# Latent attention's feature tiles inside the loop over the tables, and the low-rank products one direction ahead

## The chip, the core and the metric

The kernel runs on one core of a Trainium2 chip. The metric is device time in microseconds (us) of one execution, the median of several runs. The engines are named as in the profile: PE (TensorE, matmuls; PEld is its weight load), DVE (VectorE), ACT (ScalarE), POOL (GpSimd) and SP (SyncE, which here issues loads). PSUM is where PE's products land.

## The reference

Two blocks run one after the other. The change lies in the projection of the first block's two layers: `h @ w_in` gives latent attention's columns (query latent of 256, key-value latent of 128, rotary key of 64) and 15 tiles of 128 columns for the recurrent branch. Those are shifted over the tokens and feed, per direction, a decay, a rate and the recurrence's tables.

```python
proj = h @ w_in[li]
c_q, c_kv, k_pe, rw = _split(proj, [Q_LORA, KV_LORA, QK_ROPE, RWKV_COLS])
y_att = _mla(c_q, c_kv, k_pe, cos, sin, ...)   # RMS norms of c_q and c_kv, rotary of k_pe
u = _centred_shift(rw, mu_prev, mu_next)       # p + mu_prev*(prev-p) + mu_next*(next-p)
r, k, v, wd_f, wd_b, ad_f, ad_b, gd = _split(u, ...)
g = sigmoid(gd) @ g2
kk = heads(k * k_k); kk = kk * rsqrt(sum(kk*kk, -1) + 1e-12)
def direction(d, wd, ad, reverse):
    decay = exp(-exp(-softplus(-(w0[d] + tanh(wd) @ w2[d])) - 0.5))
    a = sigmoid(a0[d] + ad @ a2[d])
    kd = heads(k * (1.0 + (a - 1.0) * k_a))
    y = _wkv_scan(r, decay, kd, v, kk, a, reverse)
    bonus = sum(r * kd * r_k, -1) * v
```

## The kernel before

There are T = 1040 tokens (16 of them meta tokens), padded to TP = 1044. Everything here has features on the partitions and tokens along the free axis. `proj` (line 346) is called once for each layer. A **feature tile** is 128 columns of `w_in`: `load` brings the weights through SP, `parts` splits them into a high part (ACT, `pw_hi`) and a rest (DVE, `pw_lo`), and `ftile` (372) runs 3 x 8 x 3 = 72 matmuls of 348 columns into a PSUM tile `pp_ps`. That tile takes three banks and has the tag `mm`, of which there are two buffers; everything of that size shares them (`low_ps`, `kk_ps` and so on). The two remaining banks are two buffers of the tag `tp`.

`shifted` (385) evicts such a tile through ACT into `pt`, and DVE makes the shifted tile of it with three operations: L391 (times c0), L392 and L393. `plain` (441) only evicts it.

The order of the work in a layer is this. Tiles 12 and 13 (inputs of decay and rate), and then `dirs` (520): four key tiles, each with `kk` and its square on ACT; `unit_keys` (620) with the norms of the keys (`norms`) and the scaling of all four `kk` (`scaled`, 12 `kkb` products), both inside the first r tile; then the **loop over the tables**, four features f times two directions d. In it come the r tile, and per direction the low-rank products (`low`, 560: six matmuls into `low_ps`, and a tanh on ACT) for the decay `lg` and the rate `ta`, one buffer each; POOL scales `lg` (570); a scan on DVE makes `cum` (573); ACT takes two exponentials; then POOL and DVE make the tables `AR` and `BK`, which ACT's queue writes to memory (610). `BK` has one buffer, `AR` one for each direction. The bonus (612 to 618) ends a feature. After the loop come the four value tiles, `values` (643), which writes their transposes in both orders (18 row blocks, `v_sb`, two buffers), and `latent` (437) with five feature tiles: rotary key, gate (tile 14), key-value latent and two of the query latent, with norms and the gate's nine products (`g_ps`, `g_sb`) put between them by `mid`. The recurrence (`recur`, 695) begins with loads of the tables on SP and the product `aa` on PE.

Within `proj` the build orders the instructions of each engine itself, as far as dependences allow; each engine then runs its own in that order. In the recurrence the order of PE, ACT, DVE and SP is written out by hand.

Of the kernel before, what the change touches and what calls it, by code (L numbers as in the profile page):

```python
# [172 lines left out]
class K:  # L173
# [172 lines left out]
    def proj(self, li, hi, lo, p, S, psp, feed):  # L346
# [3 lines left out]
        with self.tpool(name="p_w", bufs=2) as wp, self.tpool(name="p_u", bufs=2) as up, \  # L350
# [34 lines left out]
            def shifted(j, u, mid={}):  # L385
# [5 lines left out]
                nc.vector.tensor_scalar(u, pt[:, 1:T + 1], p["c0"][:, j:j + 1], None, ALU.mult)  # L391
# [29 lines left out]
            for t in (wd, ad):  # L421
                nc.vector.memset(t[:, T:], 0.0)
            u = shifted(12, up.tile([128, T], F32, name="u"))
            nc.scalar.activation(wd[:, :T], u, AF.Tanh)
            shifted(13, ad[:, :T])
# [4 lines left out]
            with self.tpool(name="p_k", bufs=1) as kp:  # L430
                self.dirs(li, p, S, psp, up, kp, shifted, wd, ad, lw)
            with self.tpool(name="p_v", bufs=1) as vp:
                vt = [shifted(8 + f, vp.tile([128, T], F32, name=f"vt{f}", tag=f"val{f}")) for f in range(4)]
# [3 lines left out]
    def latent(self, li, p, S, psp, up, vp, shifted, ftile):  # L437

        nc = self.nc

        def plain(cols, mid=None):
            ps = ftile(cols, mid={2: mid} if mid else {})
            pt = up.tile([128, TP + 1], F32, name="pt")
            nc.scalar.activation(pt[:, :TP].rearrange("p (q n) -> p q n", q=3), ps, AF.Copy)
            return pt[:, :T]
# [20 lines left out]
        u = shifted(14, up.tile([128, T], F32, name="u"))  # L466
        gd = vp.tile([128, T], F32, name="gd")
        nc.scalar.activation(gd, u, AF.Tanh, scale=0.5)
        nc.vector.tensor_scalar(gd, gd, 0.5, 0.5, ALU.mult, ALU.add)

        def keys_end():
            ps = psp.tile([128, 3, 512], F32, name="kp_ps", tag="mm")
            c3(lambda q, c, n: nc.tensor.matmul(ps[:, q, :n], dup, kr[:, c:c + n], start=True, stop=True))
            b = vp.tile([128, T], F32, name="kp", tag="val3")
            c3(lambda q, c, n: nc.scalar.activation(b[:, c:c + n], ps[:, q, :n], AF.Copy))
            nc.scalar.dma_start(S["ckv"][1], b)


        ck = plain([(256, 128, 0)], keys_end)
# [3 lines left out]
        def gate_end():  # L483
            for c, n in TT:
                gp = psp.tile([128, 512], F32, name="g_ps", tag="tp")
                nc.tensor.matmul(gp[:n], gd[:, c:c + n], g2, start=True, stop=True)
                gs = vp.tile([128, RW], F32, name="g_sb", bufs=2)
                nc.scalar.activation(gs[:n], gp[:n], AF.Copy)
                nc.scalar.dma_start(S["g"][c:c + n, :], gs[:n])

        def ckv_end():
# [6 lines left out]


        sq = []  # L500
        for f, mid in enumerate((gate_end, ckv_end)):
            a = plain([(128 * f, 128, 0)], mid)
            x = vp.tile([128, T], F32, name=f"cq_sq{f}", tag=f"val{f}")
            nc.scalar.activation(x, a, AF.Square)
            sq.append(x)
            nc.vector.tensor_scalar(a, a, p["qn"][:, f:f + 1], None, ALU.mult)
            nc.scalar.dma_start(S["cq"][f], a)
        rq, nrq = S["rq"], S["nrq"]
        nc.vector.memset(rq, 1.0)
        sqs = psp.tile([128, 9, 2], F32, name="sqs", tag="tp")  # L510
        for i, (c, n) in enumerate(TT):
            for f in range(2):
                nc.tensor.matmul(sqs[:n, i], sq[f][:, c:c + n], ones[:, 0:2], start=f == 0, stop=f == 1)
        nc.scalar.activation(rq[:NM, 0:1], sqs[:NM, 0, 0:1], AF.Sqrt, scale=1.0 / 256, bias=self.eps["rms"][:NM])
        nc.scalar.activation(rq[:, 1:9], sqs[:, 1:9, 0], AF.Sqrt, scale=1.0 / 256, bias=self.eps["rms"])
# [4 lines left out]
    def dirs(self, li, p, S, psp, up, kp, shifted, wd, ad, lw):  # L520
# [9 lines left out]
        kt, kkt = [], []  # L530
        for f in range(4):
            k = shifted(4 + f, kp.tile([128, T], F32, name=f"k{f}"))
            kk = kp.tile([128, T], F32, name=f"kk{f}")
            nc.scalar.activation(kk, k, AF.Copy, scale=p["kk"][:, f:f + 1])
            sq = kp.tile([128, T], F32, name=f"kk_sq{f}", tag=("lg", "cum", "kd", "P")[f])
            nc.scalar.activation(sq, kk, AF.Square)
            kt.append(k), kkt.append((kk, sq))
        norms, scaled = self.unit_keys(kkt, psp, kp)
        AR = [kp.tile([128, 17, 2, 64], F32, name=f"AR{d}") for d in range(2)]
        for d in range(2):  # L540
            nc.gpsimd.memset(AR[d][:, 16 * d], 0.0)
        for f in range(4):
            r = shifted(f, up.tile([128, T], F32, name="u"), {} if f else {0: norms, 2: scaled})
            k, kk = kt[f], kkt[f][0]
            kds = []
            for d in range(2):
# [3 lines left out]
                def rv(x):  # L550
                    return x[:, ::-1] if d else x
# [1971 lines left out]
```

## Time and profile before

| | us |
|---|---|
| time, median of 3 runs (lowest, highest) | 4390.14 (4386.08, 4394.14) |
| profiled execution, its own time | 4402.54 |
| its span, first to last instruction | 4400.7 |
| PE busy / DVE / ACT / POOL in the span | 3830.7 / 2767.7 / 1869.7 / 988.2 |
| PE's mean granted clock (share of 2.4 GHz) | 0.903 |

Times of a row count from the start of the span. Busy time counts instructions that run; those that wait, branch or issue a DMA are not counted. A row of the form "A <- B" says that A's engine stood idle until B released it. The granted clock is a share of 2.4 GHz, and it has two levels: 0.50 is 1.2 GHz, 1.00 is 2.4 GHz; a value between is a stretch with both. Matmuls are pipelined, so the busy time of one is more than the distance to the next.

### The profile page before, as it was taken

Reading aid. Unit: us, or ns where it says so; the run is one execution under the profiler, and the core shown is the slowest. Engines: PE = TensorE matmul, PEld = TensorE weight load, DVE = VectorE, ACT = ScalarE, POOL = GpSimd, SP = SyncE. Lnnn points to the kernel's source line nnn. Section 1 sums busy time; section 2 is a strip of 40 time slices with the busy share of each in tenths; the row PEclk is TensorE's granted clock in tenths of the full one; section 3 lists DMA queues with packets and bytes.
Section 4 is the critical chain, followed back from the end, with each engine's and each line's share of the span. In section 5 each row is a group of like instructions: output and inputs, shape, how many; then the busy total and the mean of one; then the engine's idle time right before and its main releaser. Section 6 shows DMA issues by size and latency. Waiting matters only on the chain. (4 is left out here: it accounts for less than half of the span.)

```text
span 4400.7 us, 68329 instructions
## 1 busy us (share of the span) xinstructions
PE 3830.7 (87%) x27155; PEld 3157.1 (72%) x27155; DVE 2767.7 (63%) x4684; ACT 1869.7 (42%) x3033; POOL 988.2 (22%) x719
## 2 busy tenths in 40 slices
PE   7888897899699688897887896997898889999998
PEld 7677676786576476776776775765786677888786
DVE  7763777757698757627668577997644753333354
ACT  4323445542387543233555532876424522111232
POOL 2331124201242243311233012331422410000000
PEclk9788798999799887886988997999998899999999
DMA  4446663113499833447641043998521121111232
GB/s 154 101 129 183 160 161 108 37 54 128 160 345 346 300 102 101 115 143 172 165 125 58 1 172 131 340 335 309 181 73 29 53 97 58 48 48 43 90 126 81
DMA packets 384153, 611.94 MB, mean 139 GB/s; under 512 B 50467, under 2 KB 217602, under 8 KB 381762
## 3 DMA queue, kind: packets, MB, share of 16 engines
q1 hardware_dynamic: 278402, 485.38, 35.3%
q10 hardware_dynamic: 85200, 70.97, 5.4%
q0 software_dynamic: 20224, 51.15, 3.7%
q8 instruction: 216, 3.54, 0.3%
q14 instruction: 111, 0.91, 0.1%
HBM read 491.65 MB, written 123.45 MB: 140 GB/s over the span
## 5 line engine op out<-in xcount | busy, mean ns | idle before, releaser
L252 DVE TENSOR_TENSOR w13l<-xw,w13h 128x1024 fp32r<-128x1024 f32 x248 | 296.4, 1220 | 57.5 <-ACT w13h L251 53.9
L251 ACT ACTIVATE w13h<-xw 128x1024 fp32r<-128x1024 f32 x256 | 267.4, 1058 | 130.3 <-PE x_hp L258 76.6
L256 PE MATMUL pp_ps<-T_hi,pw_hi 128*128 128x348 f32 x912 | 309.7, 340 | 8.7 <-ACT T_hi L1752 2.9
L257 PE MATMUL pp_ps<-T_lo,pw_hi 128*128 128x348 f32 x912 | 305.4, 335 | 1.4 <-DVE T_lo L1757 1.3
L258 PE MATMUL pp_ps<-T_hi,pw_lo 128*128 128x348 f32 x912 | 304.3, 334 | 0.0
L2414 PE MATMUL f_mm<-F_hi,f_wh 128*128 128x512 f32 x704 | 222.8, 398 | 1.7 <-ACT F_hi L251 1.7
L2414 PE MATMUL f_mm<-F_lo,f_wh 128*128 128x512 f32 x704 | 222.6, 397 | 0.0
L2414 PE MATMUL f_mm<-F_hi,f_wl 128*128 128x512 f32 x704 | 222.3, 397 | 0.0
L256 PE MATMUL x_hp<-w13h,x_h 128*96 128x512 f32 x512 | 208.5, 407 | 0.1
L257 PE MATMUL x_hp<-w13l,x_h 128*96 128x512 f32 x512 | 204.7, 400 | 0.0
L258 PE MATMUL x_hp<-w13h,x_l 128*96 128x512 f32 x512 | 204.0, 398 | 0.0
L256 PEld LDWEIGHTS pp_ps<-T_hi,pw_hi 128*128 128x128 f32 x912 | 179.8, 197 | 21.8 <-issue 7.8
L257 PEld LDWEIGHTS pp_ps<-T_lo,pw_hi 128*128 128x128 f32 x912 | 179.8, 197 | 5.1 <-DVE T_lo L1757 2.6
L287 POOL TENSOR_TENSOR g_x<-g_x,g2g 128x1024 f32<-128x1024 f32 x6 | 14.3, 2385 | 750.4 <-ACT g_x L284 750.4
L258 PEld LDWEIGHTS pp_ps<-T_hi,pw_lo 128*128 128x128 f32 x912 | 179.5, 197 | 3.0 <-issue 3.0
L252 DVE TENSOR_TENSOR f_wl<-F_raw,f_wh 128x1024 fp32r<-128x1024 f32 x44 | 53.7, 1221 | 203.2 <-ACT f_wh L251 203.2
L251 ACT ACTIVATE f_wh<-F_raw 128x1024 fp32r<-128x1024 f32 x44 | 46.4, 1060 | 307.0 <-PE f_mm L2414 301.4
L1616 POOL DMA_INDIRECT d_y<-x_o,r_idx x64 | 102.8, 1606 | 312.1 <-DVE x_al L252 288.8
L825 PE MATMUL aa<-ar_p,bk_p 64*128 64x128 f32 x1088 | 134.0, 376 | 40.2 <-DVE A L827 33.6
L2414 PEld LDWEIGHTS f_mm<-F_hi,f_wh 128*128 128x128 f32 x704 | 133.1, 189 | 34.4 <-ACT F_hi L251 2.0
L2414 PEld LDWEIGHTS f_mm<-F_lo,f_wh 128*128 128x128 f32 x704 | 132.7, 189 | 32.8 <-DVE F_lo L252 0.6
L2414 PEld LDWEIGHTS f_mm<-F_hi,f_wl 128*128 128x128 f32 x704 | 132.9, 189 | 32.4
(630 smaller groups left out, 11221.3 us busy)
## 6 DMA issues: line engine op xcount, KB each, us to landing
xw<-in_moe_w SPq DMA_DIRECT2D x256, 512.0 KB
xw<-in_moe_w SPq DMA_DIRECT2D x64, 1024.0 KB
wd_raw<-in_w_down SPq DMA_DIRECT2D x44, 512.0 KB
pw_raw<-in_w_in SPq DMA_DIRECT2D x36, 512.0 KB
d_AR<-AR ACTq DMA_DIRECT2D x32, 544.0 KB
d_BK<-BK ACTq DMA_DIRECT2D x32, 544.0 KB
ar_p<-d_AR SPq DMA_DIRECT2D x68, 256.0 KB
bk_p<-d_BK SPq DMA_DIRECT2D x68, 256.0 KB
```

Source lines behind the costliest of these rows:

```text
L251: nc.scalar.activation(hi, src, AF.Copy)
L252: (lo_eng or nc.vector).tensor_tensor(lo, src, hi.bitcast(F32), ALU.subtract)
L256: mm(out, wh, xh, start=first, stop=False)
L257: mm(out, wh, xl, start=False, stop=False)
L258: mm(out, wl, xh, start=False, stop=last)
L287: e1.tensor_tensor(out[:n], out[:n], gb[:n], ALU.mult)
L825: nc.tensor.matmul(aa[d][:, h - z], bk[q, h], ar[q, h], start=True, stop=True)
L1616: nc.gpsimd.indirect_dma_start(out=y2[:, :], out_offset=bass.IndirectOffsetOnAxis(ap=si, axis=0), in_=y, in_offset=None, bounds_check=2 * ...
L2414: nc.tensor.matmul(p[:, j], a[:, k], b[:, k, 512 * j:512 * j + 512], start=st, stop=sp)
```

## The change

Five things change.

- `shifted` makes its first product (times c0) on ACT, as a second reading of the PSUM tile, and no longer on DVE.
- The key tiles take the square with the scale inside; `kk` itself is made for each feature in the loop (`scaled(f)`, one DVE operation for scaling and norm), in two buffers. `norms` comes ahead of the first r tile.
- Decay and rate are made one direction ahead of their use: `lg` gets two buffers, the next `decay` is issued as a direction begins, and the next `rate` once `ta` has been used.
- A generator `compressed` makes the four latent tiles (two of the query, the key-value latent, the rotary key); the loop takes one step of it between the two directions of each feature. The unnormed key-value latent and rotary key go to a DRAM buffer `raw`, and `latent` reads them back. The query's sums of squares are taken for each tile.
- `latent` keeps one feature tile, the gate's (14); the key-value norm and the rotated key stand between its thirds.

```diff
@@ shifted
-                nc.vector.tensor_scalar(u, pt[:, 1:T + 1], p["c0"][:, j:j + 1], None, ALU.mult)
+                nc.scalar.activation(u.rearrange("p (q n) -> p q n", q=3), ps, AF.Copy, scale=p["c0"][:, j:j + 1])
+                u = u[:, :T]
@@ proj
-                self.dirs(li, p, S, psp, up, kp, shifted, wd, ad, lw)
+                self.dirs(li, p, S, psp, up, kp, shifted, wd, ad, lw, self.compressed(p, S, psp, up, cp, ftile))
@@ compressed (new; plain is ftile, eviction to pt)
+        for f in range(2):
+            a = plain([(128 * f, 128, 0)])
+            x = up.tile([128, TP], F32, name="u")[:, :T]
+            nc.scalar.activation(x, a, AF.Square)
+            sqs = psp.tile([128, 9, 2], F32, name="sqs", tag="tp")
+            for i, (c, n) in enumerate(TT):
+                nc.tensor.matmul(sqs[:n, i], x[:, c:c + n], self.ones32[:, 0:2], start=True, stop=True)
+            nc.scalar.activation(cqs[:NM, f, 0:1], sqs[:NM, 0, 0:1], AF.Copy)
+            nc.scalar.activation(cqs[:, f, 1:9], sqs[:, 1:9, 0], AF.Copy)
+            nc.vector.tensor_scalar(a, a, p["qn"][:, f:f + 1], None, ALU.mult)
+            nc.scalar.dma_start(S["cq"][f], a)
+            yield
+        for i, cols in enumerate(([(256, 128, 0)], [(384, 64, 0), (416, 32, 64), (384, 32, 96)])):
+            nc.scalar.dma_start(S["raw"][i], plain(cols))
+            yield
@@ latent
-        kr = plain([(384, 64, 0), (416, 32, 64), (384, 32, 96)])
+        ck, kr = (vp.tile([128, T], F32, name=nm) for nm in ("ck", "kr"))
+        nc.sync.dma_start(ck, S["raw"][0])
+        nc.sync.dma_start(kr, S["raw"][1])
...
-        ck = plain([(256, 128, 0)], keys_end)
...
-        for f, mid in enumerate((gate_end, ckv_end)):
-            a = plain([(128 * f, 128, 0)], mid)
...
+        u = shifted(14, up.tile([128, TP], F32, name="u"), {0: norm, 1: rotated})
...
+        for c, n in TT:
+            gp = psp.tile([128, 512], F32, name="g_ps", tag="tp")
+            nc.tensor.matmul(gp[:n], gd[:, c:c + n], g2, start=True, stop=True)
...
@@ dirs
-            kk = kp.tile([128, T], F32, name=f"kk{f}")
-            nc.scalar.activation(kk, k, AF.Copy, scale=p["kk"][:, f:f + 1])
-            nc.scalar.activation(sq, kk, AF.Square)
+            nc.scalar.activation(sq, k, AF.Square, scale=p["kk"][:, f:f + 1])
...
+            out = kp.tile([128, TP], F32, name=nm, bufs=bufs)
...
+        def decay(f, d):
+            lg = low(wd, lw["w2"], f, d, "lg", p[f"w0{d}h"], 2)
+            nc.gpsimd.tensor_scalar(lg, lg, -0.5 * CDEC, -0.5 * CDEC, ALU.mult, ALU.add)
+            return lg
+        def rate(f, d):
+            return low(ad, lw["a2"], f, d, "ta", p[f"a0{d}h"], 1)
...
+        ahead, ta1 = decay(0, 0), rate(0, 0)
+        norms()
         for f in range(4):
-            r = shifted(f, up.tile([128, T], F32, name="u"), {} if f else {0: norms, 2: scaled})
+            k, kk = kt[f], scaled(f)
+            r = shifted(f, up.tile([128, TP], F32, name="u"))
             for d in range(2):
+                lg, ta = ahead, ta1
+                if f + d < 4:
+                    ahead = decay(f + d, 1 - d)
...
                 both(lambda o, s: nc.vector.scalar_tensor_tensor(o, s[0], 0.5, s[1], ALU.mult, ALU.mult), bk, d, (rv(ta[:, :T]), cum))
+                if f + d < 4:
+                    ta1 = rate(f + d, 1 - d)
...
+                if d == 0:
+                    next(between)
@@ unit_keys
+        def scaled(f):
+            kk = kp.tile([128, T], F32, name="kk", bufs=2)
+            for c, n in NC3:
+                rb = psp.tile([128, 512], F32, name="kkb_ps", tag="tp")
+                nc.tensor.matmul(rb[:, :n], self.pairpick[:, 128 * f:128 * f + 128], rn[:, c:c + n], start=True, stop=True)
+                nc.vector.scalar_tensor_tensor(kk[:, c:c + n], kt[f][:, c:c + n], p["kk"][:, f:f + 1], rb[:, :n], ALU.mult, ALU.mult)
+            return kk
```

## Rows read from the trace of the kernel before

**Rows 1.** Windows: us; busy PE, PEld, DVE, ACT, POOL; PEclk; DMA; GB/s.
```profile
109.00:174.00 65.00, 55.52 (x231) 37.89 (x230) 47.07 (x45) 24.42 (x27) 19.35 (x12) 0.86 0.27 65
...
174.00:281.00 107.00, 83.56 (x347) 68.54 (x346) 88.79 (x80) 36.31 (x42) 59.19 (x36) 0.71 0.56 140
...
319.00:402.00 83.00, 81.66 (x499) 74.76 (x497) 18.36 (x15) 32.74 (x50) 10.11 (x8) 0.98 0.41 142
...
1649.00:1712.00 63.00, 54.81 (x227) 37.06 (x226) 45.47 (x44) 23.95 (x27) 18.93 (x11) 0.87 0.22 56
...
1712.00:1819.00 107.00, 85.59 (x350) 69.41 (x350) 86.31 (x81) 36.19 (x43) 58.13 (x36) 0.71 0.57 142
...
1901.00:1969.00 68.00, 66.99 (x403) 60.19 (x401) 11.52 (x9) 28.91 (x46) 7.86 (x7) 0.97 0.47 157
```
**Rows 2.** Windows of tile pp_ps alone: us; busy PE, PEld, ACT; PEclk.
```profile
293.00:317.00 24.00, 24.00 (x152) 24.00 (x151) 2.05 (x2) 1.00 0.29 92
...
174.00:281.00 107.00, 43.50 (x230) 42.65 (x230) 2.06 (x2) 0.71 0.56 140
```
**Rows 3.** Line L613: duration ns min/median/max, first and last start us.
```profile
L613 DVE TENSOR_TENSOR kd<-kd,u x4: 1227/1228/1229, 173.4 to 279.6; 128x1040 f32<-128x1040 f32 x4
```
**Rows 4.** Waits, 174 to 281: us in total, times, longest.
```profile
PE bo L616 <- DVE kd L613: 14.5, 2, 7.6
...
DVE cum L573 <- POOL lg L570: 7.0, 3, 3.5
...
DVE AR L595 <- ACT P L576: 6.5, 3, 3.0
...
PE low_ps L563 <- ACT pt L390: 6.2, 1, 6.2
```
**Rows 5.** PE in time: start us, us, line, tiles, count, idle before.
```profile
125.99 2.02 PE L563 MATMUL low_ps<-s_wd,r_w 64*128 64x348 f32 x6
...
132.37 1.43 PE L638 MATMUL kkb_ps<-kk_rn,pairpick 128*128 128x348 f32 x4
...
173.52 3.84 PE L563 MATMUL low_ps<-s_wd,r_w 64*128 64x348 f32 x6 [3.90 <-ACT lg L565]
...
243.54 3.72 PE L616 MATMUL bo<-rkp,kd 128*16 128x2 f32 x18 [6.82 <-DVE kd L613]
```
**Rows 6.** DVE in time at the loop's start, same columns.
```profile
125.46 6.65 DVE L632 RECIPROCAL kk_rn<-kk_rn 128x1040 f32<-128x1040 f32 x1 [1.30 <-ACT kk_rn L631]
...
132.03 1.16 DVE L252 TENSOR_TENSOR pw_lo<-pw_raw,pw_hi 128x1024 fp32r<-128x1024 f32 x1
...
133.11 0.75 DVE L391 TENSOR_SCALAR u<-pt,pc 128x1040 f32<-128x1040 f32 x1
...
149.40 1.14 DVE L639 TENSOR_TENSOR kk<-kk,kkb_ps 128x346 f32<-128x346 f32 x2 [0.32 <-PE kkb_ps L638]
...
154.91 3.42 DVE L593 SCALAR_TENSOR_TENSOR BK<-ta,cum 128x1024 f32<-128x1024 f32 x2
```
**Rows 7.** Groups by line: busy us, mean ns, idle; L610 as rows 3.
```profile
L391 DVE TENSOR_SCALAR u<-pt,pc 128x1040 f32<-128x1040 f32 x3 | 3.1, 1018 | 0.0
...
L390 ACT ACTIVATE pt<-pp_ps 128x1044 f32<-128x1044 f32 x15 | 15.4, 1026 | 7.2 <-POOL BK L590 7.2
...
L610 ACTq EVENT_SEMAPHORE  x12: 17/3132/8101, 181.2 to 276.5; - x12
```
**Rows 8.** Tail: v_sb, g_sb as rows 3; SP, PE in time.
```profile
L686 ACT ACTIVATE v_sb<-v_ps x18: 570/597/620, 328.5 to 368.2; 128x512 f32<-128x512 f32 x16, 16x512 f32<-16x512 f32 x2
...
L686 ACT ACTIVATE v_sb<-v_ps x18: 569/594/600, 1901.1 to 1936.5; 128x512 f32<-128x512 f32 x16, 16x512 f32<-16x512 f32 x2
...
L488 ACT ACTIVATE g_sb<-g_ps x9: 571/598/604, 375.7 to 398.2; 128x512 f32<-128x512 f32 x8, 16x512 f32<-16x512 f32 x1
...
393.15 0.33 SPq L305 DMA_DIRECT2D gn_g<-in_rwkv_gn_g  x1
...
402.25 0.76 PE L825 MATMUL aa<-ar_p,bk_p 64*128 64x128 f32 x2 [1.60 <-DMA bk_p<-d_BK]
```

More of the change, by code (lines that the diff above doesn't have):

```diff
@@ L460, in latent, with norm @@
         nc.sync.dma_start(g2, self.I["rwkv_g2"][li])
-        kr = plain([(384, 64, 0), (416, 32, 64), (384, 32, 96)])
+        ck, kr = (vp.tile([128, T], F32, name=nm) for nm in ("ck", "kr"))
+        nc.sync.dma_start(ck, S["raw"][0])
+        nc.sync.dma_start(kr, S["raw"][1])
         nc.gpsimd.tensor_tensor(kr[:64], kr[:64], cos[:64], ALU.mult)
         nc.gpsimd.tensor_tensor(kr[64:], kr[64:], sin[64:], ALU.mult)
[L466 to L476, printed above, removed]
-        ck = plain([(256, 128, 0)], keys_end)
         b = vp.tile([128, T], F32, name="ck_sq", tag="val2")
         nc.scalar.activation(b, ck, AF.Square)
[L483 to L491, printed above, removed]
+        def norm():
             ps = psp.tile([128, 3, 512], F32, name="ck_ps", tag="mm")
@@ L510, in latent, with rotated @@
[L510 to L515, printed above, removed]
+        def rotated():
+            ps = psp.tile([128, 3, 512], F32, name="kp_ps", tag="mm")
+            c3(lambda q, c, n: nc.tensor.matmul(ps[:, q, :n], dup, kr[:, c:c + n], start=True, stop=True))
+            k2 = vp.tile([128, T], F32, name="kp", tag="val3")
+            c3(lambda q, c, n: nc.scalar.activation(k2[:, c:c + n], ps[:, q, :n], AF.Copy))
+            nc.scalar.dma_start(S["ckv"][1], k2)
@@ new lines, in latent @@
+        u = shifted(14, up.tile([128, TP], F32, name="u"), {0: norm, 1: rotated})
+        gd = vp.tile([128, T], F32, name="gd")
+        nc.scalar.activation(gd, u, AF.Tanh, scale=0.5)
+        nc.vector.tensor_scalar(gd, gd, 0.5, 0.5, ALU.mult, ALU.add)
+        for c, n in TT:
+            gp = psp.tile([128, 512], F32, name="g_ps", tag="tp")
+            nc.tensor.matmul(gp[:n], gd[:, c:c + n], g2, start=True, stop=True)
+            gs = vp.tile([128, RW], F32, name="g_sb", bufs=2)
+            nc.scalar.activation(gs[:n], gp[:n], AF.Copy)
+            nc.scalar.dma_start(S["g"][c:c + n, :], gs[:n])
@@ L558, in both @@
                     fn(dst[:, 16 * d, slot, 0:NM], [x[:, o:o + NM] for x in srcs])
-                def low(x, wt, out, bias):
-                    ps = psp.tile([128, 3, 512], F32, name="low_ps", tag="mm")
-                    for q in range(3):
-                        nc.tensor.matmul(ps[:, q, :348], wt[64 * d:64 * d + 64, 128 * f:128 * f + 128],
-                                         x[64 * d:64 * d + 64, 348 * q:348 * q + 348], start=True, stop=True)
-                    nc.scalar.activation(out.rearrange("p (q n) -> p q n", q=3), ps[:, :, :348], AF.Tanh, scale=0.5, bias=bias)
-                lg = kp.tile([128, TP], F32, name="lg")
-                low(wd, lw["w2"], lg, p[f"w0{d}h"][:, f:f + 1])
-                nc.gpsimd.tensor_scalar(lg, lg, -0.5 * CDEC, -0.5 * CDEC, ALU.mult, ALU.add)
                 cum = kp.tile([128, T], F32, name="cum")
@@ L628, in norms @@
                 for q, (c, n) in enumerate(NC3):
-                    nc.tensor.matmul(ss[32 * f:32 * f + 32, q, :n], self.pair32, kt[f][1][:, c:c + n], start=True, stop=True)
+                    nc.tensor.matmul(ss[32 * f:32 * f + 32, q, :n], self.pair32, sqs[f][:, c:c + n], start=True, stop=True)
             for q, (c, n) in enumerate(NC3):
@@ L632, in norms @@
             nc.vector.reciprocal(rn, rn)
-        def scaled():
-            for f in range(4):
-                for c, n in NC3:
-                    rb = psp.tile([128, 512], F32, name="kkb_ps", tag="tp")
-                    nc.tensor.matmul(rb[:, :n], self.pairpick[:, 128 * f:128 * f + 128], rn[:, c:c + n], start=True, stop=True)
-                    nc.vector.tensor_tensor(kt[f][0][:, c:c + n], kt[f][0][:, c:c + n], rb[:, :n], ALU.mult)
+        def scaled(f):
[5 more added lines that the diff above has]
+            return kk
         return norms, scaled
```

59 lines of the change are left out of this document (32 added, 27 removed).

## The prediction

> **What bounds the kernel now.** The page's chain of waits does not reach back into the two projections, so I read them by stages. First the busy time by windows [rows 1]: layer 0's projection from its last key tile to the recurrence, cut where the work changes, and the same of layer 1. The reader is to see three regimes. Ahead of the recurrence (319 to 402, 1901 to 1969) PE is busy 81.7 of 83 and 67.0 of 68 us at a granted clock of 0.97 to 0.98: PE paces this stage. In the tables' loop (174 to 281, 1712 to 1819) nothing is full: DVE 88.8 of 107, PE 83.6, POOL 59.2, ACT 36.3, and PE's clock is 0.71. Between k and loop (109 to 174) PE and DVE are busy 55.5 and 47.1 of 65.
>
> Then the price of a tile where PE paces [rows 2]: 152 matmuls in 24.00 us, 0.158 us each, so 72 are 11.4 us. Then the loop's period: the last DVE step of a feature (L613) runs four times from 173.4 to 279.6 [rows 3], so 106.2 / 3 = 35.4 us per feature. What the loop waits for stands in the list of waits [rows 4]: DVE's scan for POOL's decay (7.0 us, 3 times), DVE's table product for ACT's exponential (6.5, 3 times), PE's bonus matmuls for DVE (14.5, 2 times), PE's low-rank product for ACT's eviction of a feature tile (6.2, once). It is a chain of hand-overs with no engine full, which leaves PE room but not much.
>
> **Part 1, the tail.** Four of five feature tiles leave: 4 x 11.4 = 45.5 us of PE per layer (two sums of squares go with them, not counted). That isn't the gain, for something else is late next: the value rows. v_sb is written 18 times, from 328.5 to 368.2 in layer 0 (39.7 / 17 = 2.3 us each) and from 1901.1 to 1936.5 in layer 1 (2.1 us each); g_sb's nine follow from 375.7 to 398.2 [rows 8]. Each v_sb is evicted by ACT and written out from two buffers, and ACT waits there for the write to land, so I keep this pace. Last value matmul at E = 319 (where the windows are cut): v_sb starts at E + 9.4, its 17 steps end at E + 49, the gate's nine products fit between them (now that tile 14 comes right behind the values), the recurrence's first matmul comes at about E + 50. Today it comes at 402.25 [rows 8], E + 83. **Gain 33 us.** Also gn_g's load, which stands in front of the recurrence's loads on SP, waits for the last feature matmul (393.15 [rows 8]) and moves ahead with it. In layer 1 the value chain starts at 1901.1 as today, since tile 14 takes over as filler there; it ends at 1937, plus 3 for the last gate rows: 1940 for 1969. **Gain 29 us.** Bounds: 45 if the row writes get quicker with fewer loads beside them; 22 and 18 if the gate's products queue behind all value rows (9 x 1.2 more).
>
> **Part 2, the loop.** PE gets, per feature, one more tile and six kkb matmuls (they leave the first feature). At full clock: two tiles 22.8, 24 low-rank matmuls 4 x 2.02 = 8.1, bonus 1.9 (3.72 at half clock), kkb 1.43 x 6/4 = 2.1 [rows 5]: 34.9 us. At half clock it is near double: six low-rank matmuls took 3.84. In today's loop a tile costs between: 43.5 us of PE for 230 feature matmuls [rows 2], 13.6 us a tile. With the pauses partly filled I take 12.4 a tile, 10.5 for the low-rank products (8.1 to 15.4), 2.8 for the bonus, 2.7 for kkb: 40.8. DVE per feature: 88.8 / 3 = 29.6 busy, plus pw_lo 1.2 and three kkb products 1.6 [rows 6], plus the query scale about 0.4 (L391's operation, 0.75 off the loop [rows 6], in two of four features), minus L391's 1.0 [rows 7]: 31.8. The decay's wait (2.3 per feature) goes, because lg has two buffers and is a direction ahead; the wait for the exponential (2.2) stays, for nothing is changed in front of it: 34. So PE takes over from the hand-overs as the bound of the loop, at 40.8, and I take **41 us** for the sum, with 36 (DVE paces, PE at full clock) and 53 (see below) as ends. Three features: 3 x 5.6 = +17 us.
>
> **Part 3, the loop's start.** Today the twelve kkb products of all four features run in the first direction, the last two on DVE until 150.5, and the first BK comes at 154.9, 22.8 us after the reciprocal's end (125.46 + 6.65) [rows 6]. After the change the reciprocal is the same 6.65 us, the first scan does not wait for it, and only three kk products stand behind it. PE from the last key tile (109.1): low-rank products of the first direction 4, key norms 5 (24 short matmuls; by kkb's row 8.6 at most), r 11.4, kkb 2.1, low-rank 4, the latent tile 12.4, low-rank 4, bonus 2.8, and some 8 of waiting: 54, where 64.3 stand today (109.1 to 173.4): -10. The order of Tanh, Sqrt and Exp on ACT changes, which may cost it one more table load; that is taken into the 8. And the 14 matmuls of the second value tile that PE did ahead in the loop come later: +2.4.
>
> **Part 4, what is moved without effect.** The first product of each shift goes from DVE (0.75, in the loop 1.02 on the mean) to ACT as a second reading of PSUM: 15 a layer at 1.03 us (L390 has the same shape [rows 7]; a scale by column may add some tenths). Where k and v tiles run, PE has the next tile in the other buffer (11.4 us) and the eviction is then 2.1 instead of 1.0: hidden; if it were not, 8 tiles x 1.1 = 9 us a layer. In the loop it lies on ACT's queue, see the last rival. raw's way through DRAM: the writes are issued in features 3 and 4, the reads stand on SP in the tail behind constants: 4 DMAs, hidden by the value tiles (3 x 11.4 us); 5 us if not. kk's own ACT pass leaves k's chain; PE hides it today, so nothing.
>
> **Sum.** Layer 0: -33 + 17 - 10 + 2.4 = -23.6. Layer 1: -29 + 9.4 = -19.6 (its loop has the same numbers, rows 1). Together -43 us. The profiled execution took 4402.5 us, 12.4 over the median of the three runs, of which it would make 4359; off the median, 4390.1 - 43 = **4347 us**.
>
> **Rivals.**
> (A) PE keeps its full clock once tiles fill its pauses, and DVE paces: period 36, loop +1.8 - 10 + 2.4 = -6 a layer, sum -74: 4316 us. For it: the clock is 1.00 wherever feature tiles run on end [rows 2]. Against: PE has only two buffers of three banks for r, the latent tile and four low-rank products, and ACT empties them.
> (B) The loop takes back most: period 46, +32 - 10 + 2.4 = +24 a layer, sum -14: 4376 us. For it: PE's sum by today's prices in the loop, 2 x 13.6 for tiles, 4 x 3.3 for low-rank products (between 2.02 and 3.84), 3.7 and 3, is 47.
> (C) Slower. The place is ACT's queue. It holds the table writes, and in features 2 to 4 it stood twelve times at their semaphores, 3.1 us on the median, up to 8.1 [rows 7]; behind them are the evictions and pw_hi, which the next tile needs. Today a tile has a whole feature to spare; now two tiles and four low-rank products share two buffers in that time, PE stops at each, in order, with bonus and products queued behind, and its clock stays at 1.2 GHz after each stop. At a period of 53, +53 - 10 + 2.4 = +45 a layer, sum +28: 4418 us. It decides from 33 + 10 - 2.4 = 40.6 us of lengthening, 13.5 per feature, a period of 49 us; PE's 34.9 us of work make that at a mean clock of about 0.72, and today it is 0.71.
> The Trainium skill (TensorE: Matmul & The Clock Gate, section "A second HAM failure mode: psum-queue depth-cycling") says that a kernel which cycles through PSUM buffers lets PE idle between groups so often that the clock swings between its levels and throughput falls though the single matmul is at full speed. By that rule the swing stays in the fuller loop, which is (C) and its 4418 us; the trace shows the swing in the loop of before (0.71 in the mean), with half of the tiles that are to come.
> (D) The build orders each engine's instructions itself, within their dependences, and may put the latent tiles behind the loop: tail as today, some look-ahead gained: about 4380.
>
> **How the numbers follow.** Forecast 0.43, A 0.18, B 0.17, C 0.17, D 0.05. A measurement of this kernel can tell some 0.2% (9 us) from no change. Faster by more: forecast, A, half of B and D: 0.71. Within: the other half, 0.12. Slower: C, 0.17. The range takes in the tail's upper bound with A (4347 - 12 - 11 - 31 = 4293, rounded in to 4300) and reaches above no change into C's near side, 4405; it leaves out some 0.15.
>
> **What would show it.** Right: L613's spacing 41 us; granted clock in the loop 0.85 or more; twelve feature tiles between the last key tile's end and the last value tile's end, instead of eight; g_sb between v_sb's; the recurrence's first matmul near 379 in layer 0. Wrong: a first matmul near 402 with a loop period of 49 (C), L613 spaced 36 (A), or v_sb and g_sb still in a row, which would put part 1's pace wrong.

## The result: 29 us slower, and the profile after

The changed kernel takes 4419.2 us (median of 4 runs, 4413.0 to 4423.4), the kernel before 4390.1 us: a ratio of 1.0065 (95% interval 1.0048 to 1.0083). The forecast was 43 us faster. The profiled execution took 4418.5 us, so it lies at the median; the first profiled execution of before lay 12.4 us above its own. A second profile of the kernel before (below, 4391.2 us) has the same two projections within 2 us, so the projections can be compared.

Windows of the changed kernel, to hold against [rows 1]; columns: stretch, its length, busy us of PE, PEld, DVE, ACT and POOL with counts, PE's granted clock, DMA share, GB/s. The loop is from the first feature's last DVE step to the fourth's; then the value tiles; then the rows up to the recurrence; then the same three of layer 1:

```profile
174.00:306.00 132.00, 115.60 (x594) 98.93 (x593) 88.82 (x94) 50.94 (x59) 54.58 (x35) 0.89 0.53 126
306.00:363.00 57.00, 55.56 (x335) 55.11 (x336) 15.85 (x20) 13.07 (x15) 5.41 (x6) 0.92 0.38 124
363.00:414.00 51.00, 30.52 (x87) 14.84 (x86) 11.26 (x5) 21.06 (x34) 16.26 (x14) 0.70 0.73 235
1702.00:1842.00 140.00, 120.67 (x614) 104.53 (x612) 89.64 (x93) 51.08 (x60) 54.05 (x35) 0.88 0.50 120
1842.00:1928.00 86.00, 79.09 (x373) 63.25 (x373) 30.77 (x32) 19.08 (x27) 4.12 (x4) 0.83 0.27 80
1928.00:1984.00 56.00, 31.18 (x96) 17.25 (x96) 15.58 (x5) 23.03 (x38) 17.22 (x16) 0.73 0.60 196
```

The reader is to see two things. The loop's clock did rise (0.71 to 0.89), DVE has the same 89 us of work as before, and yet the stretch grew from 106 to about 134 us: PE stands idle for 16.4 of 132, where the forecast's 41 us a feature were PE's work without a pause. And the last 51 us ahead of the recurrence are no longer PE's: it is busy 30.5 us there, where it was busy 81.7 of 83.

The lines that answer to [rows 3] and [rows 8], of layer 0, then of layer 1 (duration min/median/max, first and last start):

```profile
L637 DVE TENSOR_TENSOR kd<-kd,u x4: 1168/1227/1229, 171.3 to 306.1; 128x1040 f32<-128x1040 f32 x4
L711 ACT ACTIVATE v_sb<-v_ps x18: 572/597/598, 357.9 to 400.8; 128x512 f32<-128x512 f32 x16, 16x512 f32<-16x512 f32 x2
L516 ACT ACTIVATE g_sb<-g_ps x9: 587/597/598, 402.3 to 414.2; 128x512 f32<-128x512 f32 x8, 16x512 f32<-16x512 f32 x1
L850 PE MATMUL aa<-ar_p,bk_p x16: 272/272/373, 413.8 to 415.7; 64*128 64x128 f32 x16
...
L637 DVE TENSOR_TENSOR kd<-kd,u x4: 1169/1224/1229, 1700.6 to 1842.1; 128x1040 f32<-128x1040 f32 x4
L711 ACT ACTIVATE v_sb<-v_ps x18: 570/597/618, 1929.7 to 1962.8; 128x512 f32<-128x512 f32 x16, 16x512 f32<-16x512 f32 x2
L516 ACT ACTIVATE g_sb<-g_ps x9: 587/597/597, 1963.8 to 1974.8; 128x512 f32<-128x512 f32 x8, 16x512 f32<-16x512 f32 x1
```

The period is 134.8 / 3 = 44.9 us in layer 0 and 47.2 in layer 1, where 41 was forecast and 35.4 stood before. All nine gate rows come behind the last value row, and the recurrence's first matmul starts at 413.81, not near 379.

From these starts each projection is cut into three: *start* (first feature matmul to the first feature's last DVE step), *loop* (from there to the fourth's) and *tail* (from there to the recurrence's first matmul). The table has them for layer 0 / layer 1 in us, the sum of all six, and the median time; the runs e1 to e16 are taken up below, and "tables on SP" means that SP issues the writes of d_AR and d_BK. What is left of a profile beside these six lay between 3590 and 3624 us in the profiled executions, so a difference of medians under some 15 us isn't always found again in the sum. It was 3610 to 3624 in the five profiles without the latent tiles in the loop, and 3590 to 3613 in those with them; why is not shown. The profiled execution of e9 lay 13 us below its median, that of e14 11 us above.

| kernel | start | loop | tail | sum | median |
|---|---|---|---|---|---|
| before | 142.3 / 153.6 | 106.2 / 104.6 | 122.7 / 151.5 | 780.8 | 4390.1 |
| before, second profile | 140.9 / 152.8 | 106.2 / 104.6 | 122.7 / 151.9 | 779.0 | |
| **changed** | 139.9 / 145.7 | 134.8 / 141.5 | 107.7 / 141.3 | 811.0 | 4419.2 |
| e1 look-ahead alone | 131.3 / 142.2 | 121.1 / 121.9 | 111.2 / 145.2 | 772.9 | 4399.1 |
| e2 move alone | 147.2 / 158.1 | 138.0 / 138.8 | 100.8 / 136.9 | 819.9 | 4419.0 |
| e3 changed, tables on SP | 133.7 / 138.6 | 112.2 / 113.8 | 109.1 / 143.3 | 750.8 | 4354.2 |
| e4 changed, four v_sb | 137.6 / 146.9 | 137.8 / 140.2 | 102.0 / 131.3 | 795.8 | 4397.2 |
| e5 before, tables on SP | 141.5 / 152.5 | 99.9 / 99.5 | 123.4 / 154.0 | 770.9 | 4394.9 |
| e6 look-ahead, tables on SP | 125.3 / 137.0 | 110.7 / 110.0 | 115.5 / 149.6 | 747.9 | 4369.3 |
| e7 = e3 + e4 | 134.0 / 141.8 | 114.9 / 113.9 | 102.1 / 131.2 | 738.0 | 4332.7 |
| e8 = e3 + gate between | 131.7 / 138.6 | 112.7 / 114.0 | 100.7 / 135.2 | 732.9 | 4345.8 |
| e9 move, tables on SP | 146.8 / 156.2 | 134.7 / 136.9 | 101.6 / 135.5 | 811.7 | 4417.0 |
| e10 = e7 + gate between | 130.5 / 139.9 | 111.4 / 113.2 | 105.3 / 126.3 | 726.7 | 4329.5 |
| e11 = e3, product on DVE | 131.1 / 140.8 | 117.0 / 115.5 | 105.5 / 143.3 | 753.2 | 4368.8 |
| e12 changed, AR issued late | 138.2 / 147.8 | 141.6 / 142.3 | 106.2 / 138.6 | 814.7 | 4427.4 |
| e13 = e9, one line moved | 147.0 / 157.7 | 134.8 / 134.8 | 102.9 / 135.9 | 813.1 | 4413.6 |
| e14 changed, AR on SP | 134.1 / 144.8 | 126.2 / 128.4 | 109.2 / 144.1 | 786.7 | 4386.5 |
| e16 = e9, decay on DVE | 147.4 / 158.0 | 118.4 / 114.2 | 101.6 / 137.4 | 777.1 | 4386.0 |

Of the changed kernel's +30 in the sum, the loops are +65.5, the tails -25.2 and the starts -10.3.

### The profile page after: what moved, and what is told of

It is laid out like the page before. It is cut to its first block, busy times and chain, and to the rows that moved or that the text cites. A ratio compares the mean times of both kernels' runs of the same rounds, so it can differ in the third digit from the quotient of the medians.

```text
span 4416.7 us, 68367 instructions
## 1 busy us (share of the span) xinstructions
PE 3814.4 (86%) x27155; PEld 3138.4 (71%) x27155; DVE 2745.0 (62%) x4656; ACT 1902.8 (43%) x3066; POOL 973.8 (22%) x719
## 5 line engine op out<-in xcount | busy, mean ns | idle before, releaser
L256 PE MATMUL pp_ps<-T_hi,pw_hi 128*128 128x348 f32 x912 | 311.5, 342 | 11.4 <-ACT lg L554 8.5
L852 DVE TENSOR_TENSOR A<-aa,cmask 128x512 f32<-128x512 f32 x136 | 87.2, 682 | 151.4 <-PE aa L850 151.2
L1641 POOL DMA_INDIRECT d_y<-x_o,r_idx x64 | 104.6, 1635 | 312.0 <-DVE x_al L252 296.1
```

Of the source, the lines that this page charges most:

```text
L256: mm(out, wh, xh, start=first, stop=False)
L852: nc.vector.tensor_tensor(A[d][:, z:z + 4], aa[d], R["mask"][d][:, None, :].to_broadcast([128, 4, 128]), ALU.mult)
L1641: nc.gpsimd.indirect_dma_start(out=y2[:, :], out_offset=bass.IndirectOffsetOnAxis(ap=si, axis=0), in_=y, in_offset=None, bounds_check=2 * ...
```

## Where the loop's time went: ScalarE's queue

One reversed direction of the changed kernel's loop, ACT in order of time (ACTq is what its queue issues), then DVE beside it:

```profile
192.39 1.13 ACT L554 ACTIVATE ta<-low_ps,phalf 128x1044 f32<-128x1044 f32 x1 [7.36 <-DVE AR L619]
192.47 1.24 ACTq L632 DMA_DIRECT2D d_BK<-BK  x2
193.82 5.58 ACTq L632 DMA_DIRECT2D d_AR<-AR  x2
199.45 1.07 ACT L598 ACTIVATE P<-cum 128x1040 f32<-128x1040 f32 x1 [5.93 <-issue]
...
192.39 2.33 DVE L595 TENSOR_TENSOR_SCAN cum<-zm,lg 128x1040 f32<-128x1040 f32 x1
200.55 3.47 DVE L617 TENSOR_TENSOR AR<-kk,P 128x1024 f32<-128x1024 f32 x2 [5.83 <-ACT P L598]
```

The look-ahead does what it says: the scan starts with no wait and ends at 194.7. But with decay ready early, the forward direction's four table writes all stand ahead of the reversed direction's exponential on ACT. Issuing them takes 1.24 + 5.58 us; the exponential comes 4.7 us after the scan's end, and DVE waits 5.83 us for it. Over this loop ACT's 25 DMA issues (22 of them table writes) add up to 29.5 us of 132. In the loop of before its 24 add up to 27.1 of 107, but there ACT also stands 42 us at 23 semaphores (the twelve of the table writes are in [rows 7]): the issues lay in idle time. Which write is slow follows its place in the group, not its table. Below, the issues of before, where d_AR goes first, and those of run e12, where d_BK does (ns min/median/max):

```profile
L610 ACTq DMA_DIRECT2D d_BK<-BK x13: 515/1925/3152, 172.9 to 280.3; - x13
L610 ACTq DMA_DIRECT2D d_AR<-AR x12: 515/518/737, 188.9 to 275.7; - x12
```

```profile
L634 ACTq DMA_DIRECT2D d_BK<-BK x14: 515/608/1303, 169.4 to 310.4; - x14
L634 ACTq DMA_DIRECT2D d_AR<-AR x12: 1192/2299/3230, 197.5 to 302.8; - x12
```

### e3, e4: the two suspects, one at a time

e3: `nc.scalar.dma_start(S[nm][d]...)` becomes `nc.sync.dma_start(S[nm][d]...)`.

> The changed kernel, the writes of d_AR and d_BK issued from SyncE's queue in place of ScalarE's; nothing else. Theory Q: the P exponential no longer stands behind four issues (two of them 2 to 3.4 us each), VectorE's AR wait of 5 to 6 us per feature goes, the period falls from 44.9 and 47.2 to 40 to 42 us; 3 gaps and 2 layers of 4 to 5 us: 4385 to 4395 us. Rival P (PE, busy in 85 to 91 % of the loop, is the limit by itself and the waits on ScalarE are slack): the period falls by less than 2 us, 4408 us or more. A third: SyncE's queue also carries the weight loads, and a write that waits for its table holds them back: PE waits for pw_raw, slower than 4419 us.

Measured: 4354.2 us, 0.9927 of before (0.9910 to 0.9944), 65 us below the changed kernel. Its two loops, as windows:

```profile
164.00:277.00 113.00, 109.82 (x591) 95.32 (x590) 95.73 (x95) 51.58 (x62) 51.58 (x35) 0.96 0.60 149
1668.00:1782.00 114.00, 112.69 (x598) 97.24 (x596) 93.35 (x94) 51.82 (x62) 50.91 (x35) 0.94 0.60 150
```

The gaps of the feature's last step are 41.0, 40.2 and 31.1 us in layer 0: near the forecast 41 in the first two (how far by luck is told below), with a shorter last feature, which prepares no next one. PE is now busy 97% of the loop: it has become the bound that the forecast took it for. DVE's waits ahead of its table product L617 fall from 14.4 us in the loop to 2.4 (8.5 of the 14.4 are put down to the exponential, 5.8 to the tile's last write landing just as the exponential ended, at 294.49). The gain is over twice the 30 us expected: PE's stops behind ACT's evictions go too (its low-rank products waited 8.1 us for the latent tile's eviction, now 2.5), and the clock rises to 0.96. Of the 60 us in the six stretches, the loops are 50 and the starts 13; the tails lose 3.

Another reading would be that the writes land sooner when SP issues them. The waits of POOL for the one BK buffer speak against it; below, first the changed kernel's loop, then e3's (us in total, times, longest):

```profile
POOL BK L580 <- DMA d_BK<-BK: 9.3, 1, 9.3
...
POOL BK L580 <- DMA d_BK<-BK: 33.1, 5, 12.9
```

POOL waits longer for the writes in e3, and the kernel is faster all the same.

The Trainium skill (DMA: Bandwidth & Descriptors, section "Issuing engines are not separate DMA queues") says that issuing from several engines saves only the sequencer's time to start a DMA, "which is usually small relative to the DMA itself". What moving the writes saved here is ACT's time to issue them, which agrees; but it was not small in this loop: one issue took up to 3.3 us, and moving them was worth 65 us. How long the transfers themselves took was not read.

e4: `name="v_sb", bufs=2` becomes `bufs=4`.

> The changed kernel with four buffers for v_sb in place of two; nothing else. Theory Q: the 18 value rows stand 2.5 us apart because each waits for the write of the row two before it to land; with four the pace falls to ScalarE's and PE's 1.2 to 1.5 us, the rows end 18 to 23 us sooner, the gate's rows follow, and both layers gain that: 4373 to 4385 us. Rival W (the transfers themselves are the limit: the DMA share is 0.73 in this stretch): the rows spread over the same time, a gain under 6 us per layer, 4407 us or more.

Measured: 4397.2 us, 1.0019 (1.0003 to 1.0034), 22 us gained where 34 to 46 were expected. The value rows of layer 0 now span 35.7 us instead of 42.9, those of layer 1 23.7 instead of 33.1; the tails are 5.7 and 10.0 us shorter. In layer 0 the stretch's DMA share is 0.81, so there the transfers are near too: of the two theories each holds half.

### e5, e6, e1: does it need the look-ahead?

e1 takes the latent tiles out of the loop and puts them back behind the values (the look-ahead, kk per feature and the first product on ACT stay); e5 and e6 are before and e1 with the writes on SP.

> The changed kernel with its latent tiles put back behind the value tiles, as in the kernel before; the look-ahead of decay and rate, kk per tile and the first product on ScalarE stay. Theory Q (the loss is made of two queues, table writes on ScalarE's queue in the loop and gate rows behind value rows in the tail): the tail is the old one, the loop carries one tile again, PE has room, and the look-ahead saves 0 to 3 us of the 35.4 per feature: 4365 to 4390 us. Rival L (the look-ahead itself does the harm: its products hold one of the two mm buffers and its evictions stand ahead of others on ScalarE): the period rises above 37 and the time is over 4400 us.

> The kernel before, the writes of d_AR and d_BK issued from SyncE's queue in place of ScalarE's; nothing else. Theory Q (the table writes harm through what stands behind them on ScalarE: with the look-ahead that is the P exponential which VectorE and GpSimd wait for, without it little): in the kernel before an issue lay in ScalarE's idle time, so this gains at most 1 to 2 us per feature, 4372 to 4392 us. Rival G (the queue is a general cost, the same 32 writes a layer): the gain is that of the changed kernel, 65 us, about 4325 us.

> The look-ahead alone (latent tiles behind the values as before) with the writes of d_AR and d_BK on SyncE's queue. Theory Q: the P exponential's waits of 5 us on the issues go, the period falls from 36.5, 43 and 41.6 to 32 to 35 us; against the look-ahead with writes on ScalarE's queue (4399) 30 to 40 us are won: 4355 to 4370 us. Rival K (with one tile the low TensorE clock, 0.72, holds the period near 40): 4385 us or more.

Measured: e1 4399.1 us (1.0026; 1.0016 to 1.0036), e5 4394.9 (0.9999; 0.9988 to 1.0009), e6 4369.3 (0.9950; 0.9933 to 0.9967). The writes' place is worth nothing in the kernel before (its loops are 5 to 6 us shorter; the total doesn't show it), 30 us with the look-ahead, 65 us with look-ahead and tiles. So the writes alone cost little; with what the change put behind them they cost much. e1's gaps are 36.5, 43.0 and 41.6 us: its loops are 15 to 17 us longer than before's, against starts 11 and tails 6 to 12 us shorter. Much of that is work that came into the loop: 276 feature matmuls in e1's first loop against 230 [rows 2], and 18 kkb products that stood in the start. In e6 it is the same: 284 feature matmuls in the first loop for e5's 220, loops 10 to 11 us longer than e5's, starts and tails 4 to 16 us shorter each, and gaps of 40.0, 33.0 and 37.7 us instead of the expected 32 to 35, at a time within the range. That e1's median is above before though its sum is 6 to 8 us below stays unexplained.

### e12, e14: the order, or the time itself

e12 puts d_AR's issue behind the next direction's exponential, still on ACT; e14 sends d_AR by SP and leaves d_BK on ACT.

```diff
+                while late:
+                    late.pop()()
...
-                for nm, t in (("AR", ar), ("BK", bk)):
+                def write(nm, t, f=f, d=d):
...
+                late.append(lambda w=write, a=ar: w("AR", a))
+                write("BK", bk)
```

> The changed kernel, all writes on ScalarE's queue as in it, but the issue of a direction's d_AR writes put behind the next direction's P exponential (d_BK's stay where they were). Theory Q in its narrow form (it is what stands behind the issues on ScalarE, the P exponential): most of the 5 to 6 us wait of the reversed direction goes, some comes back because the second exponential and the tile's eviction now stand behind them: 4385 to 4402 us. Rival (the writes' own time on ScalarE's queue counts, wherever they stand): 4412 us or more.

> The changed kernel, with d_AR's writes on SyncE's queue and d_BK's left on ScalarE's. The late issue of d_AR on ScalarE (behind the P exponential) gained nothing, 4427 us. Theory Q in its broad form (every us of issue on ScalarE's queue in this loop is on the path, wherever it stands: 29.5 us in three features): half the issues gone gives half of the 65 us, 4380 to 4395 us. Rival O (only d_AR's issues are slow, 2.3 to 3.4 us, d_BK's 0.5 to 0.7): nearly all of it, 4355 to 4368 us. Rival S (writes on SyncE's queue gain by something else than ScalarE's time): 4410 us or more.

Measured: e12 4427.4 us (1.0085; 1.0059 to 1.0111), e14 4386.5 (0.9988; 0.9979 to 0.9998). The narrow form of the theory falls. e12's ACT:

```profile
197.43 1.08 ACT L598 ACTIVATE P<-cum 128x1040 f32<-128x1040 f32 x1 [1.29 <-DVE cum L595]
197.45 4.57 ACTq L634 DMA_DIRECT2D d_AR<-AR  x2
202.07 1.07 ACT L599 ACTIVATE cum<-cum 128x1040 f32<-128x1040 f32 x1 [3.56 <-issue]
202.31 2.10 ACTq L634 DMA_DIRECT2D d_AR<-AR  x1
...
204.44 2.60 ACTq L634 DMA_DIRECT2D d_AR<-AR  x1
207.09 1.04 ACT L445 ACTIVATE pt<-pp_ps 128x1044 f32<-128x1044 f32 x1 [3.75 <-issue]
```

The exponential is early, and the same microseconds now stand ahead of the second exponential (3.56) and of the latent tile's eviction (3.75), for which PE's low-rank products wait (12.5 us in this loop, 8.1 in the changed kernel), with the bonus matmuls in order behind them. Two tiles and four low-rank products a feature leave no place on ACT where 10 us of issues lie free. e14 confirms it from the other side: without d_AR's issues half of the 65 us comes back (33), not all of it; in the six stretches it is 24 of 60.

### e2, e9, e13, e16: the move without the look-ahead

e2 is the kernel before with the move alone; e9 the same with the writes on SP; e13 moves one line of e9; e16 is e9 with decay's elementwise product on DVE:

```diff
-                nc.gpsimd.tensor_scalar(lg, lg, -0.5 * CDEC, -0.5 * CDEC, ALU.mult, ALU.add)
+                nc.vector.tensor_scalar(lg, lg, -0.5 * CDEC, -0.5 * CDEC, ALU.mult, ALU.add)
```

> The kernel before with the move alone: four latent tiles inside the loop, latent's rest behind the values as in the changed kernel; decay and rate products, kk and the first product as before. Theory Q: tail as in the changed kernel, the loop's period 46 to 50 us since the fourth tile's products add to a loop whose waits stay (35.4 + 11.4 less some of the PE waits): 4415 to 4445 us. Rival L: without the look-ahead the loop costs less than the 44.9 and 47.2 us of the changed kernel, 40 or so, and the time is below 4395 us.

> The move alone (latent tiles in the loop, no look-ahead, kk and first product as before) with the writes of d_AR and d_BK on SyncE's queue. Theory Q: in the move alone the issues stood ahead of the weight halves pw_hi and the latent tile's eviction on ScalarE (16.3 and 11.7 us of waits in the first loop); they go, but the scan still waits for decay's product (22.3 us in three features), which the look-ahead takes away: 4375 to 4395 us, above the 4354 of move, look-ahead and queue together. Rival (the look-ahead is worth nothing once the queue is free): 4350 to 4362 us.

> The move alone with the table writes on SyncE's queue (4417 us, where 4375 to 4395 was expected), and one line moved: GpSimd's zeroing of the table tile BK stands behind decay's GpSimd product instead of ahead of it. Theory P2: the move without look-ahead gained nothing from the queue since that zeroing waits for the last d_BK write to land (13.2 us at 249.1) and decay's product, and so VectorE's scan (13.24 us at 250.4), stands behind it on GpSimd; the look-ahead takes decay's product out from there. Then this gains 10 us or more per late feature, 4365 to 4390 us. Rival: the scan waits for decay's matmuls and exponential anyway, and the late table write only moves the wait to GpSimd's table products: 4408 us or more.

> The move alone with the table writes on SyncE's queue, and decay's elementwise product (before: on GpSimd, behind the zeroing of the table tile) on VectorE. The line moved in the run before did not change the order: in its trace GpSimd's zeroing still stands ahead of decay's product and waits 13.3 us for the table write. Theory P2 (that order on GpSimd is what keeps the move from gaining by the queue): the scan's waits of 29 us in the first loop fall to those for decay's matmuls and exponential, some 8 us; 20 us a layer at the most, less 1 us a direction on VectorE: 4375 to 4395 us. Rival (the wait moves on to GpSimd's table products and VectorE's table): 4405 us or more.

Measured: e2 4419.0 us (1.0076; 1.0053 to 1.0098), e9 4417.0 (1.0063; 1.0044 to 1.0082), a miss; e13 4413.6 (1.0054; 1.0037 to 1.0071), whose executed order was e9's, so it says nothing; e16 4386.0 (0.9987; 0.9976 to 0.9999). e9's POOL, and DVE behind it:

```profile
249.10 0.20 POOL L557 MEMSET BK<- 128x128 f32 x1 [13.15 <-DMA d_BK<-BK]
249.28 1.06 POOL L579 TENSOR_SCALAR lg<-lg 128x1044 f32<-128x1044 f32 x1
...
250.37 2.32 DVE L582 TENSOR_TENSOR_SCAN cum<-zm,lg 128x1040 f32<-128x1040 f32 x1 [13.24 <-POOL lg L579]
```

POOL's zeroing of the one BK buffer waits for the last write of that table to land, and decay's product stands behind it on POOL, so the scan waits too: 29.6 us in the loop. In e16 these waits are 0.3 us and 31 us are won. That is the look-ahead's use in the fuller loop: it takes decay out from behind the table's buffer. Between e16 and e3, 32 us, lie the rest of the look-ahead, kk per tile and the first product on ACT.

### e8, e7, e10: the tail

e8 calls latent's rest once the reversed copies are made, and emits one gate product and row behind each reversed value row; writes on SP.

> The changed kernel with the table writes on SyncE's queue, and in the tail the gate's nine products and rows allocated between the nine reversed value rows, in place of behind them (latent's rest is called once the reversed copies are made). This is the order that the forecast of the tail assumed. If the assumed order was the only error of that term, the 12 us of gate rows that stood behind each layer's value rows vanish under the value rows' pace: 4354 less 18 to 24, 4330 to 4336 us. Rival (rows of both kinds share the write rate, so the value rows slow by what the gate's rows take): a gain under 8 us, 4346 us or more.

> The changed kernel with both edits: the table writes on SyncE's queue and four buffers for v_sb. The two lie in different stretches, loop and tail, so their gains of 65 and 22 us add: 4330 to 4337 us. Rival (the earlier loop end moves the rows onto table transfers still under way, so the tail's gain halves): 4342 us or more.

> The changed kernel with the table writes on SyncE's queue, four buffers for v_sb, and the gate's products between the reversed value rows. With four buffers the value rows already run at 1.3 to 2 us, nearer to what the transfers give (DMA share 0.81 in the tail), so the interleaving is worth less than the 8 us it gave with two buffers: 4324 to 4332 us; if the tail is at the transfers' limit, 4333 us as without it.

Measured: e8 4345.8 us (0.9883; 0.9863 to 0.9903), e7 4332.7 (0.9862; 0.9837 to 0.9888), e10 4329.5 (0.9862; 0.9836 to 0.9889). In e8 the rows do run between each other:

```profile
L713 ACT ACTIVATE v_sb<-v_ps x18: 569/597/618, 329.6 to 375.1; 128x512 f32<-128x512 f32 x16, 16x512 f32<-16x512 f32 x2
L516 ACT ACTIVATE g_sb<-g_ps x9: 586/597/597, 356.0 to 376.5; 128x512 f32<-128x512 f32 x8, 16x512 f32<-16x512 f32 x1
```

Both tails are 8 us shorter than e3's, not 12: the value rows' pace goes from 2.5 to 2.7 us in layer 0, so part of what the gate's rows took comes back in them. Of these 16 us the median shows 8.4 (18 to 24 were expected, 8 by the rival). The gains of e3 and e4 add up in e7. e10 beats both kernels, by 1.4% the one before and by 2.0% the changed one; its 3 us over e7 can't be told from none.

### e11: the first product

e11 is e3 with the shifted tiles' first product back on DVE.

> The changed kernel with the table writes on SyncE's queue, and the shifted tiles' first product back on VectorE (15 products a layer of 0.75 to 1.0 us there in place of 1.12 us on ScalarE). Forecast's view: the product is off the path on ScalarE, so undoing it costs VectorE, at 82 % in the loop, 1 us per feature: 4356 to 4364 us. Rival (ScalarE's eviction, 1.1 us longer, holds a PSUM buffer that PE waits for): below 4350 us.

Measured: 4368.8 us (0.9954; 0.9937 to 0.9971), 15 us above e3. The loops are 4.8 and 1.7 us longer, but the six stretches together only 2.4; the rest of the 15 isn't found in them. So the sign is that of the forecast's view, the size more than it, and where most of it lies is not shown.

### e15: the kernel before, again

> The kernel before, once more under the profile, to see which stretches of its first profiled execution, 12 us above its median, were long: if the projections are 402.25 and 409.6 us again, the differences of the projections shown here stand, and the 12 us lie in the stretches behind them.

Measured: 4391.2 us; the six stretches differ from the first profile's by at most 1.4 us, and 10 of the 11 us between the two spans lie behind the start of the first layer's recurrence, more than half of the 11 after 2700 us.

## Why the prediction was wrong, point by point

**What bounds the kernel.** Right: a chain of hand-overs in the loop with no engine full. But the list of waits was read for what waits now; ACT's 42 us at semaphores [rows 7] were read as a danger (rival C) and not as the cover under which 27 us of issues lay. Two of the signs named for being right came all the same, the loop's clock (0.89) and twelve feature tiles ahead of the last value tile's end: they tell of the move, not of a gain.

**Part 2, the loop: the step that failed.** "The wait for the exponential (2.2) stays, for nothing is changed in front of it." It was changed: decay comes a direction ahead, so the exponential is due when the four writes are, and stands behind them; DVE's wait ahead of the table product went from 2.2 to 4.8 us a feature (14.4 / 3), and PE's stops came on top. The sum had a line for PE and one for DVE, and none for ACT with its issues (50.9 us busy and 29.5 of issues in 132). The term was +17 a layer; measured +28.6 and +36.9, and +6.0 and +9.2 in e3. PE as the bound was right once the writes are off ACT: the full features take 41.0 and 40.2 us for a sum of 40.8. That the numbers meet is partly luck. e3's second gap, the feature matmuls and then the low-rank products alone:

```profile
205.60:245.80 40.20, 27.78 (x166) 26.46 (x167) 3.05 (x3) 1.00 0.61 151
...
205.60:245.80 40.20, 8.07 (x24) 4.17 (x24) 4.51 (x4) 1.00 0.61 151
```

Both were cheaper than the sum had them, at a clock of 1.00: 0.167 us a matmul, so 12.0 a tile for 12.4, and 8.1 for 10.5. But 166 feature matmuls ran in that gap where two tiles have 144.

**Part 1, the tail: mis-sized, because the order of the rows was taken wrongly.** Forecast 33 and 29 (30.6 and 26.6 with the value tile's 2.4); measured 15.0 and 10.2. The rows' own pace held: 42.9 / 17 = 2.5 and 33.1 / 17 = 1.9 us for 2.3 and 2.1, starting 8.5 us behind the last value matmul (349.4) where 9.4 was taken. That the pace held is partly luck too. It was kept because ACT waits there for the write to land; but ACT's waits at its v_sb copies in layer 0, first before, then changed, are:

```profile
ACT v_sb L686 <- PE v_ps L684: 14.2, 3, 7.5
ACT v_sb L686 <- DMA d_v<-v_sb: 6.3, 3, 3.3
...
ACT v_sb L711 <- DMA d_v<-v_sb: 18.2, 11, 4.6
ACT v_sb L711 <- PE v_ps L709: 10.8, 3, 6.3
```

Before, they were for PE more than for the write; in the changed kernel the write leads, as assumed. But the gate's products did not fit between: g_sb runs from 402.3 to 414.2, 12 us, all behind. That was the lower bound (22 and 18, or 19.6 and 15.6 with the value tile's 2.4), and the right reading, though both tails gained some 5 us less still: v_ps and g_ps share the tag "tp" of one PSUM pool, and the code allocates all value products first. e8 allocates them alternately, and wins 8 of those 12 us.

**Part 3, the loop's start.** Forecast -10: measured -2.4 and -7.9, -8.6 and -15.0 once the writes are off ACT, -11.0 and -11.4 with the look-ahead alone. The sign was right, and the gain is half hidden in the changed kernel.

**Part 4.** The first product's cost was taken as nothing; it is a gain, 15 us at the median by e11, of which 6.5 are found in the loops and 2.4 in the six stretches together.

**The rivals.** C's time, 4418, is what was measured, and its place, ACT's queue with the table writes, was right. So were PE's stops behind late evictions. What it took to hold ACT was wrong: the writes wait little at their semaphores now (a median of 17 ns for the 3.1 us of [rows 7]), and it is their issue that takes ACT's time. And the clock did not stay low, it rose to 0.89. C wanted a period of 53 us; 45 to 47 were enough, because the tail gave less than half of what the forecast had put against it: that its time was met is luck in part. The Trainium skill's "A second HAM failure mode: psum-queue depth-cycling" (TensorE: Matmul & The Clock Gate), which stood behind C, says that the clock swings where PE idles between groups. The clock still swings between its two levels in the fuller loop, but with twice the tiles it is granted at 0.89 in place of 0.71, so the loss that C drew from it isn't borne out. A and B took no account of the queue; e3's loop lies between the forecast and A. D did not happen: the latent tiles ran in the loop.

**The sum.** Forecast -43, measured +30 in the six stretches. (The shares for a faster kernel add up to 0.72, not 0.71; nothing hangs on it.) The 73 us between them are the loops (31.5), the tails (32.0) and the starts (9.7). e8 has both assumptions made true, the writes off ACT and the gate's rows between the others, and takes 4345.8 us where 4347 was forecast. That is right in the direction and lucky in the number: its loops are 18 us better than forecast, its starts 6 better, its tails 19 worse.

## What to carry to other kernels

When work is moved ahead in a loop, list for each engine's queue what the moved step now stands behind, DMA issues too, with their durations; an engine at 40% busy may be full where it counts. Idle time at semaphores is cover for what is issued there, and a change that shortens the waits takes the cover away. And a tail's rows run in the order in which their PSUM buffers are allocated: read that order before counting on one group to fit between another.

## What the runs showed of the hardware

The issue of one table write took 0.51 us at the least and up to 3.5 us on ACT, up to 4.8 us on SP, the later ones of a group being the slow ones; on SP six issues run on end for 12 us:

```profile
188.78 1.28 SPq L632 DMA_DIRECT2D d_BK<-BK  x2
190.16 10.59 SPq L632 DMA_DIRECT2D d_AR<-AR  x4
```

What a long issue waits for was not tested. On SP only the next weight load stands behind them (it is issued at 200.84).

DVE's time for one shape depends on POOL: pw_lo took 1.22 us with POOL idle and up to 3.37 us beside a POOL product, on the mean 1.9 us in the changed loop and 1.22 before:

```profile
L252 DVE TENSOR_TENSOR pw_lo<-pw_raw,pw_hi 128x1024 fp32r<-128x1024 f32 x6 | 11.4, 1898 | 4.3 <-ACT pw_hi L251 4.2
```

Two long ones, each with the POOL product that ran when it began (start, us):

```profile
257.85 3.29 POOL L610 TENSOR_TENSOR BK<-kd,cum 128x1024 f32<-128x1024 f32 x1 [1.35 <-DVE kd L608]
258.83 3.41 DVE L636 TENSOR_TENSOR kd<-kd 128x1040 f32<-128x1040 f32 x1
...
300.64 3.19 POOL L610 TENSOR_TENSOR BK<-kd,cum 128x1024 f32<-128x1024 f32 x1
301.53 3.37 DVE L252 TENSOR_TENSOR pw_lo<-pw_raw,pw_hi 128x1024 fp32r<-128x1024 f32 x1
```

The DVE operation ends 1.1 us after the POOL product, at 262.24 for 261.14 and at 304.90 for 303.83, which is nearly its time alone. The other two long ones of pw_lo in this loop (1.63 and 2.71 us) end 1.1 us after a POOL product too; the short ones of pw_lo and of the kd products beside POOL began before its operation, or within 0.1 us of its start or end. The Trainium skill (SBUF — State Buffer, section "SBUF: two separate sides") says that DVE, with two SBUF inputs, and a POOL operation that reads SBUF share a pair of ports, and that the one that starts first keeps it for the whole instruction; the traces agree. No run took POOL's products away to test it.
